# Attention and pooling trunk on one core: GpSimd's 1024 column instructions cut in two during attention

## The chip, the cores and the metric

The kernel runs on one core of a Trainium2 chip. The time is device microseconds from one execution's start to its end, and the figure to be predicted is the median over several executions. TensorE (PE; its weight loads are PEld) multiplies matrices, VectorE (DVE), ScalarE (ACT) and GpSimd (POOL) work element by element, and SyncE (SP) issues most DMAs.

## The reference

The reference is one inference step of a two layer decoder trunk, d = 1024, for a prompt of 1024 positions and eight sample tokens with caches. Layer 0 mixes tokens by dilated sliding-window attention with three groups of 16 heads (windows 128, 512 and 2048 at dilations 1, 4 and 16) whose results are merged for each head slot. Layer 1 mixes by causal pooling. After each mixer comes a gated feed-forward block with a short convolution. What matters here is the merge:

```python
def merge_groups(outs):
    o = jnp.stack([t[0] for t in outs])
    m = jnp.stack([t[1] for t in outs])
    l = jnp.stack([t[2] for t in outs])
    w = l * jnp.exp(m - jnp.max(m, axis=0))
    w = w / jnp.sum(w, axis=0)
    return jnp.einsum("gbthd,gbth->bthd", o, w)
```

All products are wanted in float32. The kernel gets them from a faster matrix format by splitting every operand into a high and a low part, and by three products: high x high, high x low and low x high.

## The kernel before, in words

All of the kernel is the function `trunk`. Positions lie along the free dimension, 1032 columns (1024 of the prompt and 8 samples) in three chunks of 352, 336 and 344 columns. The features lie on the 128 partitions.

**Weights.** All weights come as a list of pieces of 128 x 1024 float32, in the order in which TensorE uses them: 72 pieces of the query, key and value projections, 8 of the output projection, then those of the feed-forward blocks and of pooling. `w_load` (line 88) issues a piece's DMA on SP's queue. `w_split` (line 96) makes the high part `w_hi` on ScalarE (line 104, a copy into the matrix format) and the low part `w_lo` as raw minus high (line 105). The low part is made on VectorE for the pieces in `quick` (the second halves of the feed-forward blocks) and on GpSimd for the others; two early pieces, 2 and 3, are given to VectorE by the caller (line 958). `w_get` hands out the next piece, and `w_ahead(1)` has the piece after it split, so that a piece is made while the one before it is used. `third` (line 73) is the number of attention pieces plus 4, so 84; it decides so far how many buffers a piece's raw data rotates through.

**Attention.** The loop at line 906 goes over 24 units, one for each of the 8 head pairs (`hp`) and 3 groups (`g` = 2, 1, 0). A unit has three weight pieces (query, key, value) times three chunks, each a run of 24 matrix products (`accumulate`, line 120, matmuls at line 125), evacuated by ScalarE (`evacuate`, line 365). While TensorE projects a unit, the unit before it attends: `attend` (line 812) makes a plan of small steps with due times, and `between` (line 843), called after each three matmuls, takes from it what is due. So the order on every engine is written by this plan, and TensorE takes projection matmuls and attention's small products in one in-order stream. The steps are:
- `scores` (452): products of keys and queries (460, 467), bias and row minimum on VectorE (461, 469), exponential on ScalarE (472).
- `probs_t` (476): transposes on TensorE (480), the high part `phl` on ScalarE (484) and its low part on VectorE (485, from PSUM).
- `pv` and `finish_o` (498, 515): probabilities times values (494), copied by ScalarE (513), summed by VectorE into the unit's output rows `og` (530).
- `transpose_v` (441): values transposed (445) and split (448 on ScalarE, 449 on VectorE).
- `pack_q` and `pack_k` (395, 409), for the next unit: high parts of queries and keys by ScalarE and VectorE (402, 403, 413, 414), and low parts, for one head by GpSimd and for the other by VectorE (404, 415). Each is an instruction of 64 partitions x 512 columns.
- Sample tokens: GpSimd multiplies cached keys with queries (650, 128 x 512) and makes the low parts of cached values (791, 128 x 512); VectorE reduces (639) and adds (776, 778, 800).

**Merge.** When the last group of a head pair has its statistics, `Merge` (line 549) puts its steps into the same plan: `weights` (567, small VectorE instructions 574 to 582 around one exponential), `rows` (584, a transpose on TensorE at 587), then for each group `fetch` (593, a DMA that spreads the weights of a group over the partitions) and `apply` (604). `apply` multiplies the group's rows (1024 columns) by the weights (607) and adds them to those of group 2 (609). For head pairs 0 to 6 this is GpSimd's work, for head pair 7 VectorE's. `store` (611) sends the merged rows out on SP's queue, or, for the last, splits them for the output projection (`attn_split`, line 854, subtraction at 856).

**After attention.** The output projection adds into the residual rows (1005, 1057) and feeds the norm of the feed-forward block; pieces 80 to 83 (the first two `up` steps) are split there. The norms at the kernel's start and here also make high and low parts: 248 and 260 on VectorE, some of 260 on GpSimd.

Of the kernel before, what the change touches and what calls it, by code (L numbers as in the profile page):

```python
# [11 lines left out]
F32 = mybir.dt.float32  # L12
# [6 lines left out]
T, NS = 1024, 8  # L19
# [28 lines left out]
def trunk(ctx: ExitStack, tc: tile.TileContext, a, out):  # L48
    nc = tc.nc
# [23 lines left out]
    third = len(pieces) + 4  # L73

    quick = set()
# [12 lines left out]
    def w_load(n):  # L88
        while nxt[0] <= min(n, len(pieces) - 1):
            i = nxt[0]  # L90
            p = more[0] if i >= third and i % 4 > 1 else wpool
            raws[i] = p.tile([128, 1024], F32, name="w_raw", tag="w_raw", bufs=2)
            nc.sync.dma_start(out=raws[i], in_=pieces[i])
            nxt[0] += 1

    def w_split(n, eng=None, load=True):
        while nxt[1] <= min(n, len(pieces) - 1):
            i = nxt[1]
            w_load(i)
            p = more[0] if more[0] is not None and i % 4 > 1 else wpool  # L100
            hi = p.tile([128, 1024], F32R, name="w_hi", tag="w_hi", bufs=2)
            lo = p.tile([128, 1024], F32R, name="w_lo", tag="w_lo", bufs=2)
            raw = raws.pop(i)
            nc.scalar.activation(hi, raw, AF.Copy)  # L104
            (eng or (nc.vector if i in quick else nc.gpsimd)).tensor_sub(lo, raw, hi.bitcast(F32))  # L105
            split[i] = (hi, lo)
            nxt[1] += 1
            if load:
                w_load(i + (4 if i >= third else 2))

    def w_get():
        i = nxt[2]
        nxt[2] += 1
        w_split(i)
        return split.pop(i)

    def w_ahead(k, load=True):
        w_split(nxt[2] - 1 + k, load=load)
# [168 lines left out]
    with ExitStack() as ph:  # L287
# [261 lines left out]
        class Merge:  # L549
# [54 lines left out]
            def apply(self, g):  # L604
                o, o2 = self.us[g].og, self.us[2].og
                eng = nc.gpsimd if self.hp < 7 else nc.vector
                eng.tensor_mul(o, o, self.cb[g])
                if g < 2:
                    eng.tensor_add(o2, o2, o)

            def store(self):
                if self.hp < 7:
# [262 lines left out]
        for f in squares(0):  # L875
            f()
        w_split(0)
        ahead = squares(1)
        for f in ahead[:2] + [norms[0].stats, norms[0].spread] + ahead[2:6]:
# [537 lines left out]
```

## Time and profile before

| | |
|---|---|
| runs of the kernel before | 2883.21, 2878.76, 2878.77 us |
| median | 2878.77 us |
| profiled execution, own time | 2875.72 us |
| its span, first to last instruction | 2873.9 us |
| mean granted TensorE clock | 0.989 |
| PE busy | 2777.4 us, 97% of the span |
| DVE, ACT, POOL busy | 1629.4, 1361.1, 1074.2 us |

The profile shows one execution. Times in the rows are microseconds from the span's start. A line number names the line of the kernel that made an instruction; `out<-in` are the program's tile names. The duration of an instruction that had to wait for a shared resource after it was begun contains that wait. Attention runs from about 60 to 1260 us, the feed-forward and pooling layers fill the rest.

### The profile page before, as it was taken

Reading aid. Unit: us, or ns where it says so; the run is one execution under the profiler, and the core shown is the slowest. Engines: PE = TensorE matmul, PEld = TensorE weight load, DVE = VectorE, ACT = ScalarE, POOL = GpSimd, SP = SyncE. Lnnn points to the kernel's source line nnn. Section 1 sums busy time; section 2 is a strip of 40 time slices with the busy share of each in tenths; the row PEclk is TensorE's granted clock in tenths of the full one; section 3 lists DMA queues with packets and bytes.
Section 4 is the critical chain, followed back from the end, with each engine's and each line's share of the span. In section 5 each row is a group of like instructions: output and inputs, shape, how many; then the busy total and the mean of one; then the engine's idle time right before and its main releaser. Section 6 shows DMA issues by size and latency. Waiting matters only on the chain. (4 is left out here: it accounts for less than half of the span.)

```text
span 2873.9 us, 46685 instructions
## 1 busy us (share of the span) xinstructions
PE 2777.4 (97%) x18109; PEld 2736.4 (95%) x18109; DVE 1629.4 (57%) x3330; ACT 1361.1 (47%) x2748; POOL 1074.2 (37%) x865
## 2 busy tenths in 40 slices
PE   6999999999999999999999999999999999999998
PEld 5999999999999998899999999999999999999998
DVE  6666656665666566755333234687755334346655
ACT  5565665566556665634223223445542233334443
POOL 4335453545354535445444434111133343331110
PEclk9999999999999999999999999999999999999999
DMA  3234332433243333537222222333422226223543
GB/s 115 61 76 135 85 98 74 124 96 96 79 120 99 93 81 108 169 111 99 74 67 74 67 74 74 110 118 118 135 88 67 74 67 76 73 68 116 173 143 92
DMA packets 203949, 277.80 MB, mean 97 GB/s; under 512 B 70272, under 2 KB 154096, under 8 KB 203728
## 3 DMA queue, kind: packets, MB, share of 16 engines
q1 hardware_dynamic: 203680, 274.80, 34.8%
q8 instruction: 142, 2.33, 0.3%
q14 instruction: 79, 0.65, 0.1%
q10 hardware_dynamic: 48, 0.02, 0.0%
HBM read 251.89 MB, written 23.34 MB: 96 GB/s over the span
## 5 line engine op out<-in xcount | busy, mean ns | idle before, releaser
L125 PE MATMUL mm<-hh,w_hi 128*128 128x352 f32 (+2 forms) x4064 | 1340.5, 330 | 9.3 <-ACT hh L256 3.3
L125 PE MATMUL mm<-hl,w_hi 128*128 128x352 f32 (+2 forms) x4064 | 1305.3, 321 | 5.0 <-DVE hl L260 5.0
L125 PE MATMUL mm<-hh,w_lo 128*128 128x352 f32 (+2 forms) x4064 | 1305.2, 321 | 1.8 <-DVE w_lo L105 1.8
L125 PEld LDWEIGHTS mm<-hh,w_hi 128*128 128x128 f32 x4064 | 769.8, 189 | 15.7 <-ACT hh L256 3.8
L125 PEld LDWEIGHTS mm<-hl,w_hi 128*128 128x128 f32 x4064 | 770.5, 190 | 7.1 <-DVE hl L260 6.5
L125 PEld LDWEIGHTS mm<-hh,w_lo 128*128 128x128 f32 x4064 | 768.9, 189 | 2.6 <-DVE w_lo L105 2.6
L105 POOL TENSOR_TENSOR w_lo<-w_raw,w_hi 128x1024 fp32r<-128x1024 f32 x212 | 514.0, 2425 | 574.2 <-ACT w_hi L104 561.3
L104 ACT ACTIVATE w_hi<-w_raw 128x1024 fp32r<-128x1024 f32 x348 | 364.7, 1050 | 290.7 <-PE mm L125 266.0
L1119 DVE SCALAR_TENSOR_TENSOR conv<-gate,convp,conv 128x336 f32<-128x336 f32 (+1 forms) x176 | 220.5, 1253 | 384.9 <-ACT conv L1117 375.9
L125 PE MATMUL mm<-gh,w_hi 128*128 128x352 f32 (+2 forms) x1056 | 340.5, 322 | 4.0 <-ACT gh L1110 2.1
L125 PE MATMUL mm<-gh,w_lo 128*128 128x352 f32 (+2 forms) x1056 | 339.9, 322 | 1.9 <-DVE w_lo L105 1.9
L125 PE MATMUL mm<-gl,w_hi 128*128 128x352 f32 (+2 forms) x1056 | 339.8, 322 | 0.3 <-POOL gl L1111 0.3
L1057 DVE TENSOR_TENSOR x<-x,mm 128x352 f32<-128x352 f32 (+2 forms) x312 | 157.1, 510 | 225.8 <-PE mm L125 225.3
L472 ACT ACTIVATE p<-p,st 128x128 f32<-128x128 f32 (+1 forms) x384 | 169.9, 443 | 201.4 <-DVE st L469 200.7
L1111 POOL TENSOR_TENSOR gl<-conv,gh 128x352 fp32r<-128x352 f32 (+2 forms) x132 | 123.5, 937 | 339.1 <-ACT gh L1110 336.1
L105 DVE TENSOR_TENSOR w_lo<-w_raw,w_hi 128x1024 fp32r<-128x1024 f32 x136 | 166.7, 1226 | 87.6 <-ACT w_hi L104 87.5
L125 PEld LDWEIGHTS mm<-gh,w_hi 128*128 128x128 f32 x1056 | 199.8, 189 | 4.6 <-ACT gh L1110 2.4
L125 PEld LDWEIGHTS mm<-gh,w_lo 128*128 128x128 f32 x1056 | 200.1, 190 | 2.2 <-DVE w_lo L105 2.2
L125 PEld LDWEIGHTS mm<-gl,w_hi 128*128 128x128 f32 x1056 | 199.9, 189 | 0.7 <-POOL gl L1111 0.7
L485 DVE TENSOR_TENSOR phl<-pt,phl 128x512 fp32r<-128x512 f32 (+1 forms) x192 | 104.7, 545 | 167.0 <-ACT phl L484 165.9
L373 ACT ACTIVATE raw<-mm 128x336 f32<-128x336 f32 (+1 forms) x216 | 144.5, 670 | 99.1 <-PE mm L125 96.7
L1102 ACT ACTIVATE gate<-mm 128x352 f32<-128x352 f32 (+2 forms) x132 | 60.2, 457 | 262.1 <-PE mm L125 262.1
(190 smaller groups left out, 3118.6 us busy)
## 6 DMA issues: line engine op xcount, KB each, us to landing
w_raw<-in_w_in SPq DMA_DIRECT2D x176, 512.0 KB
w_raw<-in_w_out SPq DMA_DIRECT2D x88, 512.0 KB
w_raw<-in_w_qkv SPq DMA_DIRECT2D x72, 512.0 KB
x<-qd SPq DMA_DIRECT2D x48, 256.0 KB
kc<-in_cache_k SPq DMA_DIRECT2D x48, 256.0 KB
vc<-in_cache_v SPq DMA_DIRECT2D x48, 256.0 KB
x<-c_d SPq DMA_DIRECT2D x42, 256.0 KB
out_new_k<-raw SPq DMA_DIRECT2D x8, 516.0 KB
```

The lines of the kernel that those rows point to most:

```text
L104: nc.scalar.activation(hi, raw, AF.Copy)
L105: (eng or (nc.vector if i in quick else nc.gpsimd)).tensor_sub(lo, raw, hi.bitcast(F32))
L125: nc.tensor.matmul(ps, l, r, start=first and i == 0, stop=last and i == n - 1)
L373: nc.scalar.activation(stream(raw[:, :T], u.g, c0, t1, which > 0), ps[:, :w].rearrange("p (s r) -> p s r", r=DILS[u.g]), AF.Copy, scale=si ...
L472: nc.scalar.activation(p[:, h, :w], p[:, h, :w], AF.Exp, bias=u.st[:, i, h, 0:1], scale=-1.0, accum_out=u.st[:, i, h, 1:2])
L485: nc.vector.tensor_sub(phl[:, :, 1, :w], ps[:, :, :w], phl[:, :, 0, :w].bitcast(F32))
L1057: nc.vector.tensor_add(xT[ct][:, c0:c1], xT[ct][:, c0:c1], ps)
L1102: nc.scalar.activation(gate[:, 2 + s:2 + e], group(tiles8(w, c), c), AF.Copy)
L1111: nc.gpsimd.tensor_sub(self.gl[f][:, s:e], conv[:, s:e], self.gh[f][:, s:e].bitcast(F32))
L1119: nc.vector.scalar_tensor_tensor(conv[:, :n], gate[:, j:j + n], cw[j], conv[:, :n], op0=ALU.mult, op1=ALU.add)
```

## The change

In `w_split` the subtraction of a piece before 84 that falls to GpSimd is made as two instructions, of columns 0 to 511 and of 512 to 1023. Other pieces, and those on VectorE, stay whole. In `apply` each product and each sum is made as two instructions of 512 columns, in the order product and sum of the first half, product and sum of the second half, on GpSimd and on VectorE alike. What is computed stays the same.

```diff
-    def w_split(n, eng=None, load=True):
+    def w_split(n, by=None, load=True):
...
             nc.scalar.activation(hi, raw, AF.Copy)
-            (eng or (nc.vector if i in quick else nc.gpsimd)).tensor_sub(lo, raw, hi.bitcast(F32))
+            eng = nc.vector if i in quick else by or nc.gpsimd
+
+            step = 512 if i < third and eng is nc.gpsimd else 1024
+            for s in range(0, 1024, step):
+                eng.tensor_sub(lo[:, s:s + step], raw[:, s:s + step], hi[:, s:s + step].bitcast(F32))
...
             def apply(self, g):
                 o, o2 = self.us[g].og, self.us[2].og
                 eng = nc.gpsimd if self.hp < 7 else nc.vector
-                eng.tensor_mul(o, o, self.cb[g])
-                if g < 2:
-                    eng.tensor_add(o2, o2, o)
+                for t in (slice(0, T // 2), slice(T // 2, T)):
+                    eng.tensor_mul(o[:, t], o[:, t], self.cb[g][:, t])
+                    if g < 2:
+                        eng.tensor_add(o2[:, t], o2[:, t], o[:, t])
```

## Rows read from the trace of the kernel before

**Rows 1.** Busy time of each engine in one period, 200 to 490 us.

```profile
core 0: us, PE busy (x) PEld busy (x) DVE busy (x) ACT busy (x) POOL busy (x), PEclk, DMA share, GB/s
200.00:490.00 290.00, 280.65 (x1927) 273.80 (x1926) 187.32 (x490) 173.24 (x436) 134.30 (x81) 0.99 0.36 98
```

**Rows 2.** Waits of TensorE's weight loads, 200 to 490 us: total, times, longest.

```profile
PEld pt L480 <- DVE phl L485: 3.6, 4, 1.1
PEld o L494 <- DVE phl L485: 2.9, 2, 2.1
PEld mt L587 <- DVE me L582: 2.5, 1, 2.5
```

**Rows 3.** Lines 105, 791, 413, 415 by source, up to 1320 us: ns minimum/median/maximum.

```profile
L105 POOL TENSOR_TENSOR w_lo<-w_raw,w_hi x82: 2347/2394/3580, 11.3 to 1312.7; 128x1024 fp32r<-128x1024 f32 x82
...
L791 POOL TENSOR_TENSOR x<-vc,x x36: 1271/1292/1542, 329.1 to 961.2; 128x512 fp32r<-128x512 f32 x36
...
L413 DVE CAST k<-raw x96: 408/965/2636, 71.7 to 1172.9; 64x512 fp32r<-64x512 f32 x96
...
L415 DVE TENSOR_TENSOR k<-raw,k x48: 689/691/2908, 72.6 to 1173.5; 64x512 fp32r<-64x512 f32 x48
```

**Rows 4.** Timelines of DVE and POOL, 198 to 205 us: start, duration, instruction.

```profile
198.59 2.12 DVE L413 CAST k<-raw 64x512 fp32r<-64x512 f32 x1
...
202.17 2.91 DVE L415 TENSOR_TENSOR k<-raw,k 64x512 fp32r<-64x512 f32 x1
...
198.04 2.39 POOL L105 TENSOR_TENSOR w_lo<-w_raw,w_hi 128x1024 fp32r<-128x1024 f32 x1 [2.54 <-ACT w_hi L104]
...
201.81 1.47 POOL L415 TENSOR_TENSOR k<-raw,k 64x512 fp32r<-64x512 f32 x1
203.24 1.28 POOL L650 TENSOR_TENSOR kc<-kc,x 128x512 f32<-128x512 f32 x1
```

**Rows 5.** Timelines of DVE, POOL and PE, 250 to 260 us.

```profile
250.22 2.76 DVE L415 TENSOR_TENSOR k<-raw,k 64x512 fp32r<-64x512 f32 x1
...
249.98 2.46 POOL L105 TENSOR_TENSOR w_lo<-w_raw,w_hi 128x1024 fp32r<-128x1024 f32 x1
252.40 1.75 POOL L650 TENSOR_TENSOR kc<-kc,x 128x512 f32<-128x512 f32 x1
...
256.79 1.46 POOL L415 TENSOR_TENSOR k<-raw,k 64x512 fp32r<-64x512 f32 x1
...
256.21 0.55 PE L494 MATMUL o<-phl,vhl 128*128 128x128 f32 x3 [1.91 <-DVE phl L485]
...
259.95 0.40 PE L460 MATMUL s<-k,x 128*128 128x256 f32 x2
```

**Rows 6.** Timelines of DVE, POOL and PE, 384 to 390 us.

```profile
385.62 1.79 DVE L402 CAST x<-raw 64x512 fp32r<-64x512 f32 x1
...
384.72 2.40 POOL L609 TENSOR_TENSOR x<-x,x 128x1024 f32<-128x1024 f32 x1
...
389.59 0.44 PE L480 MATMUL pt<-consts,p 128*128 128x128 f32 x2 [0.55 <-DVE phl L485]
```

**Rows 7.** Timelines of DVE, POOL and PE, 22 to 26 us.

```profile
22.86 2.19 DVE L260 TENSOR_TENSOR hl<-nrow,hh 128x352 fp32r<-128x352 f32 x1
...
22.04 2.63 POOL L105 TENSOR_TENSOR w_lo<-w_raw,w_hi 128x1024 fp32r<-128x1024 f32 x1
...
25.10 0.66 PE L125 MATMUL mm<-hl,w_hi 128*128 128x352 f32 x1 [1.11 <-DVE hl L260]
```

**Rows 8.** Timelines of DVE, POOL and PE, 1239 to 1246 us.

```profile
1240.11 1.21 DVE L607 TENSOR_TENSOR x<-x,cb 128x1024 f32<-128x1024 f32 x1
1241.35 3.29 DVE L609 TENSOR_TENSOR x<-x,x 128x1024 f32<-128x1024 f32 x1
...
1239.97 3.58 POOL L105 TENSOR_TENSOR w_lo<-w_raw,w_hi 128x1024 fp32r<-128x1024 f32 x1
...
1243.51 3.51 POOL L791 TENSOR_TENSOR k<-vc,k 128x512 fp32r<-128x512 f32 x2
...
1245.11 0.43 PE L125 MATMUL mm<-hh,w_hi 128*128 128x352 f32 x1 [2.57 <-DVE x L1005]
```

## The prediction, made before the changed kernel was run

> **What bounds the kernel now.** I read the busy times by stretch first, then TensorE's waits, then the engines' timelines around those waits. In a steady attention period of 290 us (two head pairs; there are nearly four such periods between 200 and 1260 us) TensorE is busy for 280.65 us [rows 1]. So about 9.3 us of each period are open to any change, and everything else is matrix work that this change leaves alone. The list of waits shows who owns that idle time [rows 2]: the split probabilities of VectorE (phl, 3.6 + 2.9 us) and the merge weights (me, 2.5 us). No weight piece stands among the first waits, and ScalarE and the DMA queues own little. The idle time comes in bursts where VectorE is late.
>
> Why it is late shows in the durations of one and the same instruction [rows 3]. The conversion at L413 takes 0.41 us at best and up to 2.64; the subtraction of L415 on VectorE 0.69 at best and up to 2.91. The timelines show with what they stretch [rows 4, 5]. At 198.59 VectorE starts an L413 that lasts 2.12 us, ending 0.28 us after GpSimd's L105 (198.04, 2.39 us). At 250.22 an L415 lasts 2.76 us beside an L105 that runs from 249.98. VectorE is held until GpSimd's instruction is over and does its own work then. The 1024 column instructions hold longest. The change halves the length of exactly these.
>
> **What the change does, part by part.** 82 subtractions of weight pieces on GpSimd (L105, pieces 0, 1 and 4 to 83) become 164, and the 35 products and sums of the merges of seven head pairs become 70. Merge seven runs on VectorE: 5 instructions become 10. No DMA is added or moved.
>
> Price of the cut: 1024 columns take a median of 2.39 us, 512 columns 1.29 us [rows 3], so a pair takes 2.58, which is 0.19 us more. For 117 pairs that is 22 us of GpSimd, spread over 1250 us in which it is busy for less than half (134.30 of 290 us [rows 1]). I cost it at nothing for the weight pieces as such: they are ordered one piece ahead, and TensorE waits for none of them [rows 2]. If that cover were gone it would be 0.19 us for each of 82. A store of merged rows on SP's queue starts later by at most a merge's five pairs, 5 x 0.19, about 1 us. Behind it stand the weight loads, which are also ordered a piece ahead, so nothing waits.
>
> The gain is in how long VectorE is held. A VectorE instruction that comes just after a 1024 column instruction has begun waits nearly 2.39 us, one that comes after a half has begun 1.29 at most. Whether VectorE gets in between two GpSimd instructions that follow without a pause decides all. At 252.40 GpSimd's L650 is recorded as begun 0.04 us before L105 ends, yet it lasts 1.75 instead of about 1.29 us, and VectorE's L415 ends at 252.98, 0.54 us after L105 [rows 5]. VectorE went first, and L650 waited. The opposite is there too: an L415 of VectorE from 202.17, 2.91 us long, was held by GpSimd's L415 (to 203.28) and also by the L650 behind it, which ran its plain 1.28 us [rows 4]. I found the first order nearly everywhere and the second in few places, so I take the first.
>
> The Trainium skill (GPSIMD Engine Reference, Instruction dispatch) says that each of GpSimd's cores begins the next instruction as soon as its own share of the one before is done, so that consecutive instructions are no barrier. By that rule two halves would hold VectorE as one piece, and the gain would be none; the row at 252.40 speaks against it, the one at 203.24 for it.
>
> Now the bursts, one by one.
>
> A, 198 to 212 us, four times. L413 is held by L105 and ends at 200.71. With halves the first is over at 198.04 + 1.29 = 199.33, and L413 ends 0.42 later at 199.75, which is 0.96 earlier. VectorE has no pause from there until the merge weights that TensorE waits for longest, so what it gains reaches TensorE. The second half can cost some of it back at the next contending instruction. Bounds: 0 (all given back) and 0.96; I take 0.9, as an L485 from PSUM (it is not held) stands between, in whose time most of the second half runs. 4 x 0.9 = 3.6 us.
>
> B, 244 to 260 us, four times. L415 from 250.22 ends at 252.98; with halves at 249.98 + 1.29 + 0.69 = 251.96, 1.0 earlier, and before it the sum of a merge (1024 columns) holds another one. The end is TensorE's wait of 1.91 us at 256.21 [rows 5]. GpSimd has no pause here, and caps the gain: its last L415, the low half of the new keys, ends at 258.25, and TensorE uses it in the scores at 259.95, so 1.70 us of room. Three pairs (two of the merge, one weight) make it 0.57 later, so TensorE can come at most 1.1 us earlier. Bounds: 0 and 1.1; I take 0.8. 4 x 0.8 = 3.2 us.
>
> C, merges of the other head pairs, three times. A conversion (L402, 385.62, 1.79 us) is held by a merge sum (384.72, 2.40 us), and TensorE idles 0.55 us for it at 389.59 [rows 6]. With halves the wait is over sooner by up to the whole 0.55; bounds 0 and 0.55, I take 0.5, as what holds it is twice the idle time. 1.5 us.
>
> D, start. L260 (22.86, 2.19 us) is held by piece 1's L105 (22.04, 2.63 us), and TensorE idles 1.11 us at 25.10 [rows 7]. It would end some 0.9 earlier (L105's first half is over near 23.6, L260 then takes about 0.5). The first piece's 0.19 lies on this stage's path. 0.7 us.
>
> E, tail, a loss. At 1240.11 VectorE does the last merge's product (1.21 us), then its sum, which L105 holds (1241.35, 3.29 us, to 1244.64), and TensorE waits 2.57 us for what stands behind it [rows 8]. GpSimd has L105 and then L791 in its queue. With halves both queues take turns: four VectorE halves of 0.69 and three GpSimd pieces of 1.29 are 6.63 us from 1240.11 on, so the end is 1246.74, 2.1 later. If L791 doesn't get in, 0.8. I take 2.1, as L791 follows L105 without a pause. The product and sum of the group before gain 0.17 us each (2 x 0.69 - 1.21) and have idle time behind them.
>
> Sum: -3.6 - 3.2 - 1.5 - 0.7 + 2.1 = **-6.9 us**. Against the profiled execution's own 2875.72 us that gives 2868.8. That execution lies 3.05 us below the median of the runs, 2878.77, so the median becomes **2871.9 us**.
>
> **Rivals.**
> 1. VectorE meets the second half. What it saves at the first it pays at the second whenever two contending instructions stand close together (in B they do: L402, L404, L413, L415 come in a row). Then A and B keep a quarter, (0.9 + 0.8) x 4 / 4 = 1.7, C and D stay at 2.2, E costs 2.1: -1.8, or 2877.0. For it: many contending instructions in B. Against: in A an uncontended one lies between.
> 2. GpSimd keeps hold of the memory through both halves. No gain; in eight bursts A and B two holds each are 0.19 us longer, 3.0, and the last sums on VectorE add 0.3: +3.3, or 2882.1. For it the row at 203.24, against it the one at 252.40. It is the case that the rule of the Trainium skill above (GPSIMD Engine Reference, Instruction dispatch) would give.
> 3. Slower: GpSimd becomes what TensorE waits for. Place: the key's low half at the end of the bursts [rows 5]. If VectorE gets in three more times of 0.69 us between halves, that and the 0.57 make it 2.64 us later, over the 1.70 of room by 0.9. In eight bursts that is 7.5, with E's 2.1 it is +9.6: 2888.4. It decides from the point where GpSimd is over 1.70 us later against TensorE. For it: GpSimd has no pause in B. Against: VectorE's contending instructions already get in once after each GpSimd instruction, so few new turns are there to take.
>
> **How the numbers follow.** The forecast has a chance of 0.60, rival 1 0.17, rival 2 0.10, rival 3 0.13. By its bounds the forecast runs from 2860 (A 0.96 and B half of the phl waits of rows 2, 3.25, four times each, C whole at 1.65, D 0.7, E 0.8: -18.4) to 2877, where rival 1 takes over. Its likeliest part, 2866 to 2875, is where most of its chance lies. The range **2860 to 2883** takes in rivals 1 and 2 and leaves out rival 3 and a sliver below. A measurement can tell about 0.2%, 5.8 us, from no change: that is 2873.0 and 2884.5. Of the forecast 0.52 lies below 2873.0, 0.08 above it; with rivals 1 and 2 the middle has 0.35, rival 3 gives 0.13.
>
> **What would show it.** Right: L105 twice as often in attention at about 1.29 us; the longest L413 and L415 of VectorE near 1.7 to 2.0 us instead of 2.6 to 2.9; TensorE's waits for phl and me down from 9.0 to some 6 us a period; the wait near 1242 longer by about 2. Wrong: VectorE's longest durations unchanged (rival 2), shorter but more of them with the same sum (rival 1), or TensorE waiting for GpSimd's keys before scores (rival 3).

## The result and the profile after

The changed kernel took 2860.84 us (median; 2855.86 to 2862.2), the kernel before on the same chip 2880.78: a ratio of 0.9931 (95% interval 0.9919 to 0.9942), 19.9 us less. The forecast was 6.9 us less, so sign and mechanism came out and the size did not. The profiled execution took 2860.84 us with a span of 2859.0. Span against span the gain is 14.9 us; the other 5 us is that the profiled execution of before lay 5 us below this median of its runs (five by now; the first three had 2878.77).

Busy time of the engines, from the page of the changed kernel:

```profile
PE 2778.1 (97%) x18109; PEld 2741.0 (96%) x18109; DVE 1606.4 (56%) x3335; ACT 1362.1 (48%) x2748; POOL 1102.1 (39%) x982
```

GpSimd has 27.9 us more (117 more instructions, at 0.19 us forecast 22), VectorE 23.0 less for the same arithmetic. TensorE does the same work.

The instructions of the lines in question up to 1320 us (the line numbers of after are 4 or 5 higher: L105 is L109, L413 is L417, L415 is L419, L485 is L489, L587 is L591), to be read against [rows 3]:

```profile
L109 POOL TENSOR_TENSOR w_lo<-w_raw,w_hi x166: 1262/1291/2402, 11.4 to 1316.7; 128x512 fp32r<-128x512 f32 x164, 128x1024 fp32r<-128x1024 f32 x2
...
L417 DVE CAST k<-raw x96: 407/940/2015, 71.5 to 1158.0; 64x512 fp32r<-64x512 f32 x96
...
L419 DVE TENSOR_TENSOR k<-raw,k x48: 687/1652/1679, 72.4 to 1160.1; 64x512 fp32r<-64x512 f32 x48
```

The longest L419 fell from 2.91 to 1.68 us, the longest L417 from 2.64 to 2.02. But the median L419 rose from 0.69 to 1.65: VectorE now meets an instruction of GpSimd more often, and each meeting is shorter.

What TensorE makes of it in the period of [rows 1] and [rows 2]: busy time, and the waits of its weight loads.

```profile
200.00:490.00 290.00, 282.89 (x1935) 276.82 (x1935) 186.05 (x490) 174.82 (x438) 142.17 (x109) 0.99 0.35 98
```

```profile
PEld mt L591 <- DVE me L586: 2.3, 1, 2.3
PEld o L498 <- DVE phl L489: 2.2, 1, 2.2
...
PEld pt L484 <- DVE phl L489: 1.6, 3, 0.8
```

The three of [rows 2] go from 9.0 to 6.1 us. The place where it is easiest to see is the burst of [rows 4]. TensorE's waits there before:

```profile
201.36 0.44 PE L480 MATMUL pt<-consts,p 128*128 128x128 f32 x2 [0.48 <-DVE phl L485]
...
207.54 0.55 PE L494 MATMUL o<-phl,vhl 128*128 128x128 f32 x3 [0.58 <-DVE phl L485]
...
212.21 0.29 PE L587 MATMUL mt<-consts,me 128*48 128x128 f32 x1 [2.18 <-DVE me L582]
```

The same burst in the timelines of DVE, POOL and PE of the changed kernel:

```profile
197.49 1.01 DVE L417 CAST k<-raw 64x512 fp32r<-64x512 f32 x1
...
199.97 1.67 DVE L419 TENSOR_TENSOR k<-raw,k 64x512 fp32r<-64x512 f32 x1
...
196.93 2.72 POOL L109 TENSOR_TENSOR w_lo<-w_raw,w_hi 128x512 fp32r<-128x512 f32 x2 [2.54 <-ACT w_hi L104]
199.62 1.48 POOL L655 TENSOR_TENSOR kc<-kc,x 128x512 f32<-128x512 f32 x1
...
209.49 0.29 PE L591 MATMUL mt<-consts,me 128*48 128x128 f32 x1 [2.07 <-DVE me L586]
```

The L417 that took 2.12 us beside a whole L105 takes 1.01 beside the halves. Of TensorE's three waits only the last is left.

After attention nothing changes: from TensorE's weight load 8500 (just behind the handover to the feed-forward layers) to the end it is 1536.1 us before and 1536.2 after. The table counts what lies between its weight loads 230 and 8500 (attention and the handover), in the one profiled execution of each run, all in us. *Held*: what VectorE's four kinds of pack instructions (240 in all, 144 in runs 7, 8 and 11) took above 0.42 us (conversions) and 0.69 us (subtractions). *Waits*: time in which TensorE had neither matmul nor weight load. *Half clock*: time at a granted clock of 1.2 GHz instead of 2.4.

| kernel | ratio of medians | held | waits | half clock | length |
|---|---|---|---|---|---|
| before | 1 | 123.9 | 54.3 | 27.3 | 1273.1 |
| the change | 0.9931 [0.9919, 0.9942] | 102.1 | 39.6 | 34.1 | 1258.3 |
| 1 weights alone | 0.9957 [0.9945, 0.9969] | 104.1 | 45.9 | 34.1 | 1265.8 |
| 2 merge alone | 0.9999 [0.9990, 1.0008] | 116.6 | 50.7 | 37.5 | 1273.5 |
| 3 second half first | 0.9923 [0.9909, 0.9937] | 101.3 | 37.1 | 30.7 | 1254.4 |
| 4 last merge whole | 0.9911 [0.9899, 0.9923] | 102.8 | 37.7 | 20.5 | 1251.7 |
| 5 as 4, quarters | 0.9925 [0.9913, 0.9938] | 66.9 | 41.4 | 30.7 | 1259.0 |
| 6 as 4, all of GpSimd's cut | 0.9879 [0.9864, 0.9894] | 76.2 | 31.5 | 17.1 | 1241.5 |
| 7 before, key high halves on ScalarE | 0.9883 [0.9870, 0.9897] | 46.1 | 31.1 | 20.5 | 1243.0 |
| 8 as 4, key high halves on ScalarE | 0.9860 [0.9847, 0.9874] | 43.3 | 25.3 | 23.9 | 1237.2 |
| 9 as 4, pack's low halves cut | 0.9918 [0.9905, 0.9930] | 90.9 | 34.9 | 20.5 | 1246.3 |
| 10 as 4, cache instructions cut | 0.9922 [0.9908, 0.9935] | 89.6 | 32.8 | 30.7 | 1250.7 |
| 11 6 and 8 together | 0.9845 [0.9831, 0.9858] | 36.0 | 22.5 | 17.1 | 1231.8 |
| 12 before, only small ones cut | 0.9928 [0.9915, 0.9942] | 96.2 | 36.9 | 30.7 | 1253.5 |

Two readings of it are used below. The length less the waits and less half of the half clock time is 1200 to 1205 us in every row, so these two make nearly all of the difference between the kernels. And with less held time there is mostly less waiting; run 5 is the clear exception (the change and run 4, with held times 0.7 us apart, stand the other way round too).

### The profile page after: what moved, and what is told of

Read it like the earlier page. It is cut to its first block, busy times and chain, and to the rows that moved or that the text cites. A ratio compares the mean times of both kernels' runs of the same rounds, so it can differ in the third digit from the quotient of the medians.

```text
span 2859.0 us, 46821 instructions
## 1 busy us (share of the span) xinstructions
PE 2778.1 (97%) x18109; PEld 2741.0 (96%) x18109; DVE 1606.4 (56%) x3335; ACT 1362.1 (48%) x2748; POOL 1102.1 (39%) x982
## 5 line engine op out<-in xcount | busy, mean ns | idle before, releaser
L109 POOL TENSOR_TENSOR w_lo<-w_raw,w_hi 128x512 fp32r<-128x512 f32 (+1 forms) x294 | 532.8, 1824 | 565.5 <-ACT w_hi L104 564.1
L109 DVE TENSOR_TENSOR w_lo<-w_raw,w_hi 128x1024 fp32r<-128x1024 f32 x136 | 166.5, 1225 | 87.8 <-ACT w_hi L104 87.8
L489 DVE TENSOR_TENSOR phl<-pt,phl 128x512 fp32r<-128x512 f32 (+1 forms) x192 | 104.6, 545 | 165.8 <-ACT phl L488 164.7
```

The costliest lines, as they stand in the source:

```text
L109: eng.tensor_sub(lo[:, s:s + step], raw[:, s:s + step], hi[:, s:s + step].bitcast(F32))
L489: nc.vector.tensor_sub(phl[:, :, 1, :w], ps[:, :, :w], phl[:, :, 0, :w].bitcast(F32))
```

## The experiments

All compute what the kernel before computes. The theory under test: a pack instruction of VectorE that starts while GpSimd is in an instruction is held until that one is over, so the length of GpSimd's instructions sets how late VectorE, and with it TensorE, becomes.

**1. Weights alone.** `apply` is put back.

```diff
-                for t in (slice(0, T // 2), slice(T // 2, T)):
+                for t in (slice(0, T),):
```

> Leaves the merge's products and sums whole and cuts only the weight pieces. Theory (VectorE is held for the length of GpSimd's instruction): the weight pieces hold VectorE more often than the merges, so about two thirds of the 18 to 20 us gained remain, 10 to 14 us under the kernel before; the wait of 0.55 us at the merges of the odd head pairs (389 us) comes back, those near 201 and 207 us stay away. Rival (TensorE gets the first half of a low part sooner): the whole gain remains, 17 us or more, since merges don't feed TensorE.

Measured 0.9957, 12.0 us below the 2878.61 of before. Hit. The waits at 201 and 207 stay away, the one near 389 (whole merge sum) is back.

**2. Merge alone.** `w_split` is put back.

```diff
-            step = 512 if i < third and eng is nc.gpsimd else 1024
+            step = 1024
```

> Cuts only the merge's products and sums; the weight pieces stay whole. Theory (VectorE is held): 4 to 8 us under the kernel before, waits near 237 and 389 us go, those near 201 and 207 us are as before; the longest key subtraction on VectorE is back at 2.7 us or more. Rival (first half of the low part sooner): no gain at all, within 2 us of the kernel before.

Measured 0.9999: no gain, a miss. The waits behind the merges do become shorter, by 0.84 us near 237 and 0.77 near 389 for instance. But in its timelines VectorE, free earlier, runs into the next whole weight subtraction:

```profile
401.20 2.71 POOL L109 TENSOR_TENSOR w_lo<-w_raw,w_hi 128x1024 fp32r<-128x1024 f32 x1
...
401.70 2.49 DVE L417 CAST k<-raw 64x512 fp32r<-64x512 f32 x1
...
404.59 0.44 PE L484 MATMUL pt<-consts,p 128*128 128x128 f32 x2 [1.48 <-DVE phl L489]
```

The kernel before has no wait there, and the same new one stands in the next two periods. The tail loses as well: VectorE's halves of the last merge stand beside a whole L109, and the wait of [rows 8] grows from 2.57 to 4.84 us:

```profile
1246.43 0.66 PE L129 MATMUL mm<-hh,w_hi 128*128 128x352 f32 x1 [4.84 <-DVE x L1010]
```

In the table the waits are 3.6 us less than before, and 10.2 us more at half clock cost 5.1. So the zero has three parts: the new waits, the tail, where VectorE's own halves lose as in run 4, and the clock. With the tail's wait taken out (1.48 us in run 1, 4.84 here, 3.76 in the change, 2.57 before) the gains are about 10.9 alone, 2.3 alone and 21.1 together: still not a sum. That a whole weight piece next in GpSimd's queue is what spoils the merge's part fits these timelines and is no rule (run 12).

**3. Second half first.** Does TensorE gain because the first half of a piece is there sooner? Then the reverse order must lose it.

```diff
-            for s in range(0, 1024, step):
+            for s in reversed(range(0, 1024, step)):
```

> As the changed kernel, but of each weight piece the columns 512 to 1023 are made first, so that the part that TensorE uses first is ready 1.29 us later than in the changed kernel. Theory (VectorE is held): the holds are the same, so within 2 us of the changed kernel, 17 to 21 us under the kernel before. Rival (first half sooner): the gain from the weight pieces is gone, less than 8 us under the kernel before, and TensorE waits for w_lo.

Measured 0.9923, 23 us below before (17 to 21 were expected), its interval overlapping that of the change. The gain doesn't come from an earlier first half.

**4. Last merge whole on VectorE.**

```diff
-                for t in (slice(0, T // 2), slice(T // 2, T)):
+                for t in ((slice(0, T // 2), slice(T // 2, T)) if self.hp < 7 else (slice(0, T),)):
```

> As the changed kernel, but the last head pair's merge, on VectorE, stays whole. Theory (both queues take turns in the tail): the wait near 1230 us, 3.76 us in the changed kernel, falls to between 2.6 and 3.2 us, and the kernel is 0.5 to 1.5 us faster than the changed one. Rival (the tail's loss comes from the weight piece's halves, not from the merge's): the wait stays above 3.5 us and the time is unchanged.

Measured 0.9911, its interval just overlapping that of the change: by the medians 5.8 us faster, where 0.5 to 1.5 were expected. First the changed kernel's tail, to be read against [rows 8], then that of this run (DVE, POOL and PE timelines):

```profile
1225.52 0.67 DVE L612 TENSOR_TENSOR x<-x,cb 128x512 f32<-128x512 f32 x1
1226.23 1.67 DVE L614 TENSOR_TENSOR x<-x,x 128x512 f32<-128x512 f32 x1
1227.82 1.75 DVE L612 TENSOR_TENSOR x<-x,cb 128x512 f32<-128x512 f32 x1
1229.61 1.63 DVE L614 TENSOR_TENSOR x<-x,x 128x512 f32<-128x512 f32 x1
...
1225.54 3.48 POOL L109 TENSOR_TENSOR w_lo<-w_raw,w_hi 128x512 fp32r<-128x512 f32 x2
1228.99 3.39 POOL L796 TENSOR_TENSOR k<-vc,k 128x512 fp32r<-128x512 f32 x2
...
1231.71 0.66 PE L129 MATMUL mm<-hh,w_hi 128*128 128x352 f32 x1 [3.76 <-DVE x L1010]
```

```profile
1222.53 2.21 DVE L614 TENSOR_TENSOR x<-x,x 128x1024 f32<-128x1024 f32 x1
...
1225.21 0.43 PE L129 MATMUL mm<-hh,w_hi 128*128 128x352 f32 x1 [1.49 <-DVE x L1010]
```

Halves take turns with GpSimd's pieces, and each of VectorE's last three is held once; whole, only the sum is held, once, by a half. The wait goes from 3.76 to 1.49 us (2.6 to 3.2 were expected). These 2.27 us are the edit's. The lengths in the table differ by 6.6, and most of that is less time at half clock (20.5 against 34.1 us, worth 6.8): 3.4 us of it followed the change's tail wait, the rest lies elsewhere and varies. This is the base of most of the next runs.

**5. Quarters.**

```diff
-            step = 512 if i < third and eng is nc.gpsimd else 1024
+            step = 256 if i < third and eng is nc.gpsimd else 1024
...
-                for t in ((slice(0, T // 2), slice(T // 2, T)) if self.hp < 7 else (slice(0, T),)):
+                for t in ([slice(s, s + T // 4) for s in range(0, T, T // 4)] if self.hp < 7 else (slice(0, T),)):
```

> Against the run with head pair 7's merge whole on VectorE (ratio to the kernel before 0.9911 [0.9899, 0.9923], about -25 us), this run cuts the weight subtractions and the merge of head pairs 0 to 6 into four instructions of a quarter of the columns. From 1.29 us at half and 2.39 at whole a quarter is worked out at 0.74 us, so one piece or product takes 2.96 us of GpSimd instead of 2.58, and the longest hold of VectorE by one of them is 0.74 instead of 1.29. Theory (VectorE is held for what is left of one GpSimd instruction, so the length of an instruction sets the price): a pack instruction that meets a quarter takes at most about 1.4 us for its 0.69 and 1.1 for its 0.41; the waits that remain at half length shrink again, by less than the first cut gave because GpSimd's other 512-column instructions (1.29 us) still hold: 3 to 7 us faster than that run, ratio 0.9885 to 0.990. Rival (a price for each GpSimd instruction, or GpSimd's own 15% longer work making the next pieces and key low halves late): no faster or up to 6 us slower than that run, ratio 0.991 to 0.993.

Measured 0.9925, in the rival's range: no faster than run 4 although VectorE is held 36 us less. The waits of TensorE's weight loads for GpSimd's low half of the keys, up to 1320 us, in the changed kernel (one, at the start) and in this run (one more in each of four periods):

```profile
PEld s L464 <- POOL k L419: 3.2, 1, 3.2
```

```profile
PEld s L464 <- POOL k L419: 7.3, 5, 3.2
```

The first of the new ones, in this run's timelines of POOL and PE:

```profile
249.39 3.66 POOL L109 TENSOR_TENSOR w_lo<-w_raw,w_hi 128x256 fp32r<-128x256 f32 x4
253.01 1.29 POOL L655 TENSOR_TENSOR kc<-kc,x 128x512 f32<-128x512 f32 x1
254.26 1.27 POOL L419 TENSOR_TENSOR k<-raw,k 64x512 fp32r<-64x512 f32 x1
...
255.58 0.51 PE L464 MATMUL s<-k,x 128*128 128x256 f32 x2 [0.74 <-POOL k L419]
```

GpSimd's four quarters take 3.66 us where the whole took 2.46 [rows 5], it has no pause behind them, and its key low half holds up the scores: it ends at 255.53, where it ended at 255.35 before, and TensorE is there 5.1 us earlier (254.84 against 259.95). TensorE waiting for GpSimd's keys is the mechanism of the prediction's rival 3, brought on by twice the cuts.

**6. All of GpSimd's instructions of attention at half length.** Besides the 1024 column ones, the low halves of queries and keys, the products on cached keys and the low halves of cached values (each 512 columns) run as two of 256.

```diff
-                        nc.gpsimd.tensor_mul(kc[i - 1], kc[i - 1], qb[i - 1])
+                        for j in range(2):
+                            nc.gpsimd.tensor_mul(kc[i - 1][:, j], kc[i - 1][:, j], qb[i - 1][:, j])
...
-                nc.gpsimd.tensor_sub(lo, self.vc[n], hi.bitcast(F32))
+                for j in range(2):
+                    nc.gpsimd.tensor_sub(lo[:, j], self.vc[n][:, j], hi[:, j].bitcast(F32))
```

and in `pack_q` and `pack_k` the subtraction of head 0 runs over `t` in two parts.

> Against the run with head pair 7's merge whole on VectorE (ratio 0.9911), GpSimd's remaining long instructions of attention (the 512-column low halves of queries, keys and cache values and the cache key products, 1.29 us each) run as two of 256 columns, an estimated 0.74 us each. Theory (hold by instruction length): what still holds VectorE for up to 1.3 us now holds it for 0.74; the weight halves and merge halves stay at 1.29, so a part of the remaining holds shrinks: 1 to 4 us faster than that run, ratio 0.9895 to 0.991. Rival (GpSimd's chain key high half, key low half, scores is what ends the remaining waits; each cut adds 0.19 us to it): 1 to 3 us slower than that run, ratio 0.9915 to 0.992.

Measured 0.9879, 9.3 us below run 4: the theory's sign, more than twice its size. Of this, 2.8 us of the profiled execution lie after attention, where it has 6.8 us less at half clock than run 4 (run 11 has the same 2.8).

**7. Key high halves to ScalarE, on the kernel before, nothing cut.**

```diff
-                nc.vector.tensor_copy(keys[h][own, 0, t], raw[own, t])
+                nc.scalar.activation(keys[h][own, 0, t], raw[own, t], AF.Copy)
```

> The kernel before, with no cut at all, and one thing moved: the key's high half of a head (64x512, 0.41 us on VectorE where nothing holds it, about 0.63 on ScalarE by the neighbouring copy of the same size) is rounded by ScalarE. VectorE has half as many pack instructions to be held in, and GpSimd's low half no longer waits for a VectorE instruction. Theory (the waits of attention come from VectorE's pack instructions held by GpSimd's whole-width ones): the waits near 201 and 207 shorten or vanish without any cut, VectorE's held time falls from 124 us to under 90; 5 to 14 us faster than the kernel before, ratio 0.995 to 0.998. Rival (the pack on the whole sets the end, on whichever engine it runs): ScalarE, busy 60% of a period with softmax exponentials behind it, gets 15 us more a period and makes the probabilities late: no faster or up to 10 us slower, ratio 1.000 to 1.0035.

Measured 0.9883, 33 us below before: far beyond the theory's 5 to 14, and more than the whole change. The moved instruction's row, and TensorE's waits of 200 to 490 us:

```profile
L413 ACT ACTIVATE k<-raw x96: 613/630/637, 70.0 to 1140.9; 64x512 fp32r<-64x512 f32 x96
```

```profile
PEld pt L480 <- DVE phl L485: 1.9, 2, 1.1
PEld mt L587 <- DVE me L582: 1.2, 1, 1.2
```

On VectorE the same instruction took from 0.41 to 2.64 us [rows 3]; on ScalarE each of the 96 takes 0.61 to 0.64, and 54 of them begin while GpSimd is in an instruction. The Trainium skill (SBUF — State Buffer, Who interferes with whom) says that some of VectorE's instructions use a pair of ports shared with GpSimd, which one of the two holds for a whole instruction, and that ScalarE has its own; these rows agree. The run frees VectorE of 63 us of held time and of 96 x 0.41 = 39 us of its own work alike, and doesn't part the two. (Run 8 frees the same 39 us and gains 14. If that work is worth the same in both runs, at least 19 of the 33 us here are the hold; that it is, no run shows.) It shows that the pack on VectorE was behind much of TensorE's waiting, and that ScalarE has room for it.

**8. The same move on the kernel of run 4.**

> The same move of the key's high half to ScalarE, on top of the halved weight pieces and merge (head pair 7's merge whole): ratio to compare with is 0.9911. Theory: with halves the holds are at most 1.3 us, so the move brings less than on the kernel before: 0 to 6 us faster than that run, ratio 0.989 to 0.991. Rival (ScalarE becomes the late engine): slower than that run by 2 to 10 us, ratio 0.992 to 0.9945.

Measured 0.9860, 14 us below run 4, beyond the theory's 0 to 6. ScalarE's longer work costs less than the move brings: the waits of the table fall by 12.4 us.

**9 and 10. The two parts of run 6, one at a time.** 9 cuts only the pack's low halves, 10 only the cache instructions.

> On top of the halved weights and merge with head pair 7's merge whole (0.9911), only the low halves of queries and keys on GpSimd (64x512, 1.29 us) run as two of 256 columns. The run that cut these and the cache instructions stood at 0.9879, 10 us below. Theory that the low halves hold the other head's VectorE instructions (both belong to one pack, so they run side by side every time): most of the 10 us is here, ratio 0.988 to 0.9895. Rival (the cache instructions, which fall anywhere, are what is met): little here, ratio 0.990 to 0.9915. Adding 0.19 us per low half to the chain that ends in the scores speaks for the rival.

> The complement: only the products on the key cache and the low halves of the cache's values on GpSimd (128x512, 1.29 us) run as two of 256 columns, on the same base (0.9911). By the theory that the pack's own low halves hold most: ratio 0.990 to 0.9915. By its rival: 0.988 to 0.9895. If both parts give about half, 0.9895 each, every shortened kind counts in proportion to how often it runs.

Measured 0.9918 and 0.9922, each just outside the ranges on record: neither differs from run 4 (0.9911) by more than its interval. Neither the theory nor its rival put "nothing from either, 9 us from both" on record. The table says part of it: the held time falls in both (90.9 and 89.6 from 102.8), the waits too (by 2.8 and 4.9 us), but in run 10 10.2 us more at half clock eat its 4.9. One execution each doesn't tell more.

**11. Runs 6 and 8 together.**

> Key high halves on ScalarE (run on the halved kernel: 0.986) and GpSimd's remaining 512-column instructions halved (0.9879 without that move), together. Theory: both shorten the same waits, so the sum is far from additive; what is left of waits of attention in the run with the move is mostly the matrix of the merge's factors (0.87 us) and cache values (0.66 to 0.96): 0 to 5 us below the run with the move alone, ratio 0.9843 to 0.986. Rival (GpSimd, 13% longer, makes key low halves late now that the high halves come later from ScalarE): 0.986 to 0.9885.

Measured 0.9845, 45 us below before and, by the median, below every other run here; it lies 4 us below run 8, as the theory had it, and the two intervals overlap. In the stretch of 70 to 1238 us of before, the change, run 7 and this one (columns as in [rows 1]):

```profile
70.00:1238.00 1168.00, 1122.91 (x7696) 1095.35 (x7695) 762.57 (x1967) 693.02 (x1750) 526.12 (x317) 0.99 0.37 101
```

```profile
70.00:1238.00 1168.00, 1134.91 (x7755) 1109.73 (x7754) 753.30 (x1984) 698.12 (x1756) 560.90 (x430) 0.99 0.37 103
```

```profile
70.00:1238.00 1168.00, 1142.59 (x7844) 1117.25 (x7843) 667.56 (x1897) 760.21 (x1861) 542.89 (x325) 0.99 0.37 105
```

```profile
70.00:1238.00 1168.00, 1150.60 (x7923) 1126.72 (x7923) 665.13 (x1909) 763.84 (x1868) 599.67 (x629) 1.00 0.37 105
```

TensorE gets 227 more matmuls done in the same stretch. GpSimd works 74 us longer for it: an engine off the path may be made slower, so long as it lets go sooner.

**12. Only the small instructions cut, on the kernel before** (weights and merge whole).

> The kernel before with weights and merge whole and only GpSimd's 512-column instructions (low halves of queries, keys and cache values, cache key products) halved. Theory (a wait vanishes only if no long instruction is met next; with 2.4-us instructions left, VectorE that gets past a small one meets a large one, as in the run with the merge alone halved, 0.9999): little, ratio 0.9975 to 1.000. Rival (every shortened kind brings its own part, independent of the others): the same 10 us as on the halved kernel, ratio 0.9955 to 0.997.

Measured 0.9928, 20.7 us below before, as much as the change and beyond both expected ranges. The theory's form of run 2, that short instructions bring nothing while long ones are left, falls as a rule: it holds for the merge and not for the small ones. Nor do the parts add up (here 20.7, on run 4 9.3).

## Why the prediction was right, and by how much it was off

**The mechanism.** Each sign that the prediction named came: L109 twice as often at 1.29 us, the longest L417 and L419 at 2.02 and 1.68, the three waits of a period down from 9.0 to 6.1, and a longer wait in the tail, though by 1.2 us and not by about 2. VectorE gets in between two of GpSimd's instructions: counted over both traces, 124 of 130 held pack instructions before, and 137 of 139 after, were held by one instruction of GpSimd, the rest by two. In some 62 of the 124 and 92 of the 137 another GpSimd instruction stood less than 0.2 us behind the one that held, so these decide. The prediction cited the Trainium skill (GPSIMD Engine Reference, Instruction dispatch) for its statement that a core of GpSimd begins the next instruction as soon as its own share of the one before is done. That two halves would therefore hold VectorE as one piece was the prediction's own reading of it, its rival 2; the traces decide against that reading.

**Rival 1** (the second half is met as well) is half true: 139 held instances instead of 130. But the held time fell by 21.8 us, and the waits with it, where that rival would have left 1.8 us of gain.

**The terms.** TensorE's matmuls are the same in both traces and in the same order, so the start of each one after can be set against before. Steps of that difference, summed by burst (us; a minus is a gain):

| term | forecast | waits gone or added | with what followed, up to the next burst |
|---|---|---|---|
| A, four bursts | -3.6 | -6.4 | -1.7 |
| B, four bursts | -3.2 | -10.4 | -8.7 |
| C, three merges | -1.5 | -2.3 | -0.8 |
| D, start | -0.7 | -1.3 | -0.3 |
| E, tail | +2.1 | +1.2 | -0.3 |
| not in the sum | 0 | -1.7 | -3.1 |
| sum | -6.9 | | -14.9 |

- A held in kind and was too small: each burst lost two short waits, of some 0.7 and 0.8 us, and the sum had counted one hold of 0.96. Then three of the four gave 1.5 us back each, as a stretch at half clock followed the wait that was left (below).
- B was mis-sized most, by a misread row. The cap of 1.1 us took the scores at 259.95 to use GpSimd's last L415 of the burst, which ends at 258.25. `pack_k` begins with the columns 512 to 1023, and the first scores of a unit use keys of these, so they need the L415 before it. That one ends at 255.35, and the room is 4.60 us instead of 1.70. The trace of before shows it itself in the third burst, where the scores start while the last L415 is still running (POOL at 254 us; POOL and PE at 840 us):

```profile
254.10 1.25 POOL L415 TENSOR_TENSOR k<-raw,k 64x512 fp32r<-64x512 f32 x1
...
840.29 1.29 POOL L415 TENSOR_TENSOR k<-raw,k 64x512 fp32r<-64x512 f32 x1
...
840.33 0.40 PE L460 MATMUL s<-k,x 128*128 128x256 f32 x2
```

  With no such cap TensorE came 3.0 to 3.4 us earlier in the second to fourth burst, where several waits shrink and the sum had counted one: those at 527.8, 540.4 and 547.5 us, 0.86, 1.60 and 1.91 us in the matmuls' rows, became 0.05, 0.48 and 0.80. In the first burst little was gained, and the reason is the order that rival 2 rests on. The timelines of DVE, POOL and PE of after, against [rows 5]:

```profile
251.76 1.99 DVE L417 CAST k<-raw 64x512 fp32r<-64x512 f32 x1
...
250.96 1.29 POOL L419 TENSOR_TENSOR k<-raw,k 64x512 fp32r<-64x512 f32 x1
252.21 1.25 POOL L655 TENSOR_TENSOR kc<-kc,x 128x512 f32<-128x512 f32 x1
...
254.26 0.55 PE L498 MATMUL o<-phl,vhl 128*128 128x128 f32 x3 [2.00 <-DVE phl L489]
```

The conversion from 251.76 is held by L419, to 252.25, and by the L655 behind it, to 253.46: one of the two such cases in this trace. The wait stays, and half clock follows it at 255 us.
- C: all of the 0.55 us wait vanished, and 0.77 with it, but VectorE, free earlier, met the next piece at 400, 690 and 980 us, which gave back 0.4 to 0.7 each time. That is run 2's effect in small.
- D: the wait at 25 us fell by 1.3, of which 0.3 was left by 79 us.
- Not in the sum: 0.8 at 80 us, where an L415 held by an L105 delayed the scores of the first unit, and 0.8 at 592 us, a wait for phl like those of A. The rest is a stretch at half clock at 348 us that only the trace of before has.
- E went as worked out, taking turns included (the rows of run 4), and cost 1.2 instead of 2.1: VectorE's first half went free and the other three were held for 0.9 to 1.1 us each, where the sum had three whole pieces of 1.29.

Another step was wrong in itself: C and the short waits of A were priced from the matmul's rows. The weight load in front of it waits longer. In the trace of before, the PEld timeline at the wait of [rows 6]:

```profile
389.59 0.20 PEld L480 LDWEIGHTS pt<-consts,p 128*128 128x128 f32 x2 [0.83 <-DVE phl L485]
```

  0.83 us here against 0.55 in the matmul's row, and 0.77 us was gained when it went. So each short wait is worth about 0.25 us more than the matmul's row says; with 49 waits over 0.25 us before and 33 after that is some 4 us, an estimate. The sum also didn't agree with the prediction's own sign that waits would go from 9.0 to some 6 us a period: 3 us times four is 12, and its terms came to 2.1 a period. Setting the sum against the total of [rows 2] would have shown it.

That the measured 2860.84 us still lies in the range, 0.84 us above its lower end of 2860, is luck more than working: that end gave B 3.25 us a burst, half of the phl waits, against the working's own cap of 1.1.

**Rival 3** (GpSimd becomes what TensorE waits for) had no place in the change. It was priced with the same misread 1.70 us of room; its mechanism came in run 5.

**Open.** Why some waits of 2 us are followed by half clock and others not (below); why the parts of run 6 don't add up; how much of run 7 is the hold and how much VectorE's own work.

## What to carry to other kernels

Where VectorE is on the path beside GpSimd, the length of GpSimd's instructions is a price that no busy share shows: look for a VectorE instruction whose duration spreads from its minimum to several times that, cut what holds it, and stop where GpSimd's own chain becomes late (here at quarters). Look first whether the held instruction can run on ScalarE, which isn't held: one moved line gave more than all the cuts of the change. Leave VectorE's own instructions whole where they stand beside GpSimd's on the path (run 4's tail), and measure cuts in company, as their parts did not add up here.

## What the runs showed of the hardware that was not expected

**Clock.** After some of TensorE's longer waits the granted clock falls to half (1.2 of 2.4 GHz) for some us, after others not. The same code in both traces, first the 2.2 us before the merge's transpose, then 3.4 us from 1.1 us after its start; before, then after:

```profile
209.90:212.10 2.20, 0.13 (x1) 0.00 (x0) 1.68 (x10) 1.00 (x3) 0.00 (x0) 1.00 0.00 0
213.30:216.70 3.40, 3.40 (x24) 3.38 (x24) 1.60 (x8) 2.99 (x8) 1.46 (x1) 1.00 0.43 163
```

```profile
207.20:209.40 2.20, 0.22 (x2) 0.00 (x0) 1.68 (x10) 1.00 (x3) 0.00 (x0) 1.00 0.00 0
210.60:214.00 3.40, 3.40 (x14) 3.40 (x14) 1.57 (x8) 2.47 (x7) 1.50 (x2) 0.50 0.43 163
```

TensorE was idle alike and is busy throughout alike, but at 1.00 in the one and 0.50 in the other, with 24 and 14 matmuls done: some 1.7 us lost. Their places differ from kernel to kernel, and their total (17 to 38 us at half clock, so 9 to 19 us lost) varies as much as many of the effects studied here. A difference of a few us between two profiles can be this alone.

**Whom GpSimd holds.** Not every instruction of VectorE is held. Of the pack instructions of before (conversions and subtractions from SBUF) 128 began well inside a GpSimd instruction of over 0.7 us; 123 lasted until it was over. VectorE's reductions of cached products (L639, which read SBUF too) were not held: all 96 took 0.41 to 0.43 us, 34 of them begun inside such an instruction. Nor were those of L485, which read PSUM (0.41 to 0.43 us for each of the 104 of 256 columns, 44 begun inside). ScalarE's copies are not held either (run 7). Cutting costs GpSimd little: 1.29 us for 512 columns against 2.39 for 1024, and a median of 0.74 for 256 in run 5.
